# Attention's weights times values: one 32-bit product replaced by three products of 16-bit high and low parts

## The chip, the cores and the metric

The kernel runs on one core of a Trainium2 chip. A core has a matrix engine (PE, with its weight loads shown apart as PEld), a vector engine (DVE), a scalar or activation engine (ACT), a general engine (POOL), and a queue engine that starts most transfers (SP). The metric is the device time of one execution in microseconds (us); lower is better. Results of the PE go to eight PSUM banks, everything else lies in SBUF, and larger tensors in DRAM.

## What is computed

Two layers over 1024 tokens of width 1024. Each layer normalises its input, projects it (`h @ w_in`) and runs three groups of heads: a bidirectional gated delta rule (GDN, 6 heads), latent attention (MLA, 6 heads) and RWKV-7 (4 heads). Their outputs are concatenated, gated, projected by `w_out` and added to the input. The change is in the attention; cut to that part the reference reads:

```python
def mla_branch(cols, positions, q_norm_g, w_uq, kv_norm_g, w_ukv):
    ...
    kv = (rms_norm(cols['mla_ckv'], kv_norm_g) @ w_ukv).reshape(b, l, MLA_HEADS, MLA_NOPE + MLA_V)
    k_nope, v = kv[..., :MLA_NOPE], kv[..., MLA_NOPE:]
    ...
    def attend(q_blk):
        s = jnp.einsum('bqhd,bkhd->bhqk', q_blk, k)
        p = jax.nn.softmax(s, axis=-1)
        return jnp.einsum('bhqk,bkhd->bqhd', p, v)
```

## The kernel before, in words

**Two streams.** A layer's work is split in two streams that share the engines. One is the scan: first RWKV (`rwkv`, 193 rounds of the scheduler loop `chain`), then GDN (`gdn`, 279 rounds). GDN has three pairs of heads and per pair eight preparations (`gdn_prep`, with the chunk inversion `invert`, lines 904 to 985) and sixteen steps (`gdn_step`, L1106 to L1130). The other is the dense stream (`dense_work`): the input projection (`in_tiles`, L378 to L380 through the helper `mm3`), then MLA (`mla`), then the parts of the output projection that are ready (`out_part`, `out_open`). What is left of the output projection (`out_proj`) runs after both, on the whole machine.

**What sets the order.** The dense stream is a generator. Each `yield us` announces how many us of PE work the next piece is reckoned at. In every round `chain` calls `tick(dense / len(turn))` once per running thread, so that a round moves the dense stream's goal by `DENSE_R` us during RWKV and by `DENSE_G` us during GDN, and pulls pieces until the goal is reached. Whatever the dense stream has left when GDN is done is pulled at once. On top of that `order` ties PE instructions of the two streams to each other: a dense matmul stands behind the scan's last matmul of `LEAD` = 4 rounds ago, and the scan's matmuls behind the last dense one. The framework then lays out each engine's instructions in one fixed order, and every engine works through its own in that order.

**MLA.** Per layer there are six units: three pairs of heads (`pr`) times two halves of 512 queries (`nh`). A unit first gets its queries and keys (`mla_q`, `mla_k`) and the maximum of the scores (`mla_max`, L1740 on the PE and the reduction L1741 on DVE). Then `mla_main` goes over eight blocks `t` of 128 keys. For each block and each of the two heads `h`, `scores` makes a 128x512 block of scores with three matmuls (L1773 to L1775) in a bank from the pool `A`, and ACT takes the exponential (L1777, into a buffer named `mp`). POOL adds it to the running sum `acc[h]` (L1779, tiles `md`). One block later `values` multiplies: the 128x64 block of values of head `h` is the stationary operand, the 128x512 exponentials the moving one, and the two heads' results go to partitions 0 to 63 and 64 to 127 of one bank, `po`, which stays taken for the whole unit (L1784). Both operands are plain 32-bit there. `mla_tail` sums `acc` over the partitions with a matmul by ones (L1816), copies both banks out (L1818, L1819), takes reciprocals by way of DRAM, and scales (L1830, L1835). The values come from `mla_v`, which copies each projected block out of PSUM (L1685).

**Buffers.** The pool `A` has three PSUM banks, and nearly every dense matmul takes its bank there. The tag `mp` has five buffers of 128x512; `out_part` loads the residual into the same tag (L1878), adds a product to it on DVE (L1883) and stores it (L1884), 16 times a layer. In the GDN step, `gs_e` (L1111, POOL) holds the decayed state.

The middle of `mla_main` before the change, the part that the prediction speaks of most:

```python
            pT = self.T("mp", [128, 512], F32, 5)
            nc.scalar.activation(pT, ps, AF.Exp)
            if t:
                nc.gpsimd.tensor_tensor(out=acc[h], in0=prev[h] if t == 1 else acc[h], in1=pT, op=ALU.add)
            return pT

        def values(t, pT):
            for h in range(2):
                self.did = nc.tensor.matmul(po[NR[h]], lhsT=vv[:, t, 2 * pr + h], rhs=pT[h], start=(t == 0), stop=(t == 7))
```

## Time and profile before

| what | value |
|---|---|
| median of three runs | 2501.53 us (2496.85 to 2509.19) |
| the profiled execution: its own time | 2507.43 us |
| the profiled execution: span from first to last instruction | 2505.7 us |
| mean granted PE clock in it | 0.951 |
| busy: PE / DVE / ACT / POOL | 91% / 66% / 55% / 34% of the span |
| attention, layer 0 and layer 1 | about 780 to 1190 us and 2000 to 2415 us |

A row of the groups reads: line, engine, operation, tiles written and read, shapes and type, number of instructions, then busy time and the mean of one in ns, then the engine's idle time just before them and what ended it. On the PE the end of a matmul is modelled: the time that one takes from the next is the distance between their starts, which the timeline shows (its first column is the start in us, the second the duration). A 32-bit matmul appears there as two instructions, its two passes. Line numbers are those of the kernel before; the change shifts lines after 424 by three to nineteen.

### The profile page before, as it was taken

To read this page: it belongs to the slowest core of one execution; us is meant where nothing else is said; L and a number is where in the kernel's file an instruction comes from. 1 tells how busy PE (TensorE), PEld (TensorE's weight loads), DVE (VectorE), ACT (ScalarE), POOL (GpSimd) and SP (SyncE) were. 2 spreads that over 40 slices of the span, in tenths; PEclk is the share of its full clock that TensorE was granted. 3 is DMA by queue.
4 is the path that set the end of the run, shared out by engine and by line. 5 is a ranking of instruction groups with operands and counts; after the bars stand their busy time and mean duration, and the time that the engine had idled before them with its cause. 6 is when DMAs were issued, how large, how long until landed. Compare 5 with 4: busy or idle time off the path is not lost.

```text
span 2505.7 us, 54928 instructions
## 1 busy us (share of the span) xinstructions
PE 2274.3 (91%) x21524; PEld 1386.8 (55%) x21524; DVE 1643.2 (66%) x3706; ACT 1386.2 (55%) x3077; POOL 844.7 (34%) x1079
## 2 busy tenths in 40 slices
PE   5999989899899999988989999898988999998988
PEld 3455645555575555544754555555546755554556
DVE  6557778655577765775345676877456776667655
ACT  5567656655555554555245775666565456555541
POOL 1222323223224544554012232342232255445430
PEclk9999999899899989999999999998998899899999
DMA  4121222213251111102212222222224411111041
GB/s 127 46 66 51 69 64 77 56 61 120 98 171 43 37 52 31 32 25 90 93 63 56 56 68 70 66 67 56 90 88 138 128 41 32 50 38 32 21 145 68
DMA packets 140338, 174.09 MB, mean 69 GB/s; under 512 B 37072, under 2 KB 95536, under 8 KB 140080
## 3 DMA queue, kind: packets, MB, share of 16 engines
q1 hardware_dynamic: 139936, 170.19, 22.5%
q8 instruction: 170, 2.79, 0.5%
q14 instruction: 88, 0.72, 0.1%
q0 software_dynamic: 144, 0.39, 0.1%
HBM read 106.88 MB, written 39.04 MB: 58 GB/s over the span
## 4 chain that ended last, share of the span: by engine, by line
PE 56%; DVE 19%; ACT 8%; issue 6%; POOL 6%; DMA 5%; SPq 0%; POOLq 0%; ACTq 0%; DVEq 0%
PE pa L378 5%; PE pa L1784 5%; PE pa L379 5%; PE pa L380 5%; PE pb L923 4%; DMA wf<-in_w_in_dram 3%; PE pa L1740 3%; POOL wl L539 2%; PE pa L1773 2%; DVE cacc L735 2%; PE pe L840 2%; PE pe L1348 2%; PE pe L966 2%; PE pa L1774 1%; PE pc L1114 1%
## 5 line engine op out<-in xcount | busy, mean ns | idle before, releaser
L378 PE MATMUL pa<-h,wh 128*128 128x512 f16 x864 | 335.6, 388 | 1.4 <-DVE h L491 1.4
L380 PE MATMUL pa<-h,wl 128*128 128x512 f16 x864 | 333.7, 386 | 0.8 <-POOL wl L539 0.8
L379 PE MATMUL pa<-h,wh 128*128 128x512 f16 x864 | 334.5, 387 | 0.0
L949 DVE TENSOR_TENSOR z<-pb,c 128x256 f16<-128x256 f32 (+1 forms) x320 | 155.7, 487 | 166.4 <-PE pb L923 163.4
L927 ACT COPY bdz<-z 64x256 f16<-64x256 f16 (+1 forms) x384 | 173.4, 455 | 123.1 <-DVE z L949 99.3
L1779 POOL TENSOR_TENSOR md<-md,mp 128x512 f32<-128x512 f32 x144 | 192.1, 1336 | 141.6 <-ACT mp L1777 132.4
L539 POOL TENSOR_TENSOR wl<-wf,wh 128x512 f16<-128x512 f32 x108 | 128.1, 1203 | 234.8 <-ACT wh L538 200.7
L954 ACT CAST x<-pb 128x256 f16<-128x256 f32 (+1 forms) x320 | 135.1, 422 | 103.8 <-PE pb L923 102.7
L1784 PE MATMUL pa<-mp,mv 128*64 128x512 f32 x384 | 188.4, 631 | 0.0
L967 ACT CAST xT<-pe 128x512 f16<-128x512 f32 x256 | 151.1, 590 | 57.1 <-PE pe L966 56.0
L1412 POOL TENSOR_TENSOR rs_e<-rs_z,rw_em 64x128 f32<-64x128 f32 x120 | 57.2, 491 | 287.1 <-DVE rs_z L1439 257.5
L1741 DVE TENSOR_REDUCE mmx<-pa 128x1 f32<-128x512 f32 x192 | 130.9, 686 | 32.5 <-PE pa L1740 29.2
L928 DVE COPY bdz<-z 64x256 f16<-64x256 f16 (+1 forms) x384 | 139.0, 365 | 17.4 <-PE pe L966 5.7
L1777 ACT ACTIVATE mp<-pa 128x512 f32<-128x512 f32 x192 | 114.4, 596 | 63.6 <-PE pa L1775 60.3
L923 PEld LDWEIGHTS <-bdgh 128*128 128x128 f16 x1920 | 93.4, 100 | 88.8 <-issue 56.8
L923 PEld LDWEIGHTS <-xT 128*128 128x128 f16 x1600 | 77.5, 100 | 97.2 <-issue 55.8
L380 PEld LDWEIGHTS <-wl 128*128 128x128 f16 x864 | 85.2, 99 | 81.6 <-issue 6.0
L735 DVE SCALAR_TENSOR_TENSOR cacc<-raw,dv,cacc 128x512 f32<-128x512 f32 x144 | 124.1, 884 | 6.9 <-ACT raw L728 3.5
L378 PEld LDWEIGHTS <-wh 128*128 128x128 f16 x864 | 91.0, 105 | 66.0 <-issue 11.4
L923 PE MATMUL pb<-z,xT 128*128 128x64 f16 x1600 | 109.3, 197 | 16.7 <-DVE z L949 12.7
L529 DVE TENSOR_REDUCE wc<-wf 128x1 f32<-128x512 f32 x108 | 71.7, 680 | 71.8 <-DMA wf<-in_w_in_dram 71.5
L379 PEld LDWEIGHTS <-wh 128*128 128x128 f16 x864 | 85.3, 99 | 60.1 <-issue 8.4
(462 smaller groups left out, 5677.0 us busy)
## 6 DMA issues: line engine op xcount, KB each, us to landing
wf<-in_w_in_dram SPq DMA_DIRECT2D x54, 512.0 KB
q_d<-cacc SPq DMA_DIRECT2D x18, 512.0 KB
rw_ka<-rw_kr SPq DMA_DIRECT2D x32, 256.0 KB
rw_ka<-rw_ak SPq DMA_DIRECT2D x64, 128.0 KB
gate_d<-gate SPq DMA_DIRECT2D x16, 512.0 KB
wof<-in_w_out_dram SPq DMA_DIRECT2D x16, 512.0 KB
xp_d<-mp SPq DMA_DIRECT2D x32, 256.0 KB
xo<-xp_d SPq DMA_DIRECT2D x16, 512.0 KB
```

The source lines that it names most:

```text
L378: self.did = nc.tensor.matmul(out, lhsT=lh, rhs=rh, start=(first and idx == 0), stop=False)
L379: self.did = nc.tensor.matmul(out, lhsT=lh, rhs=rl, start=False, stop=False)
L380: self.did = nc.tensor.matmul(out, lhsT=ll, rhs=rh, start=False, stop=(last and idx == n - 1))
L539: nc.gpsimd.tensor_tensor(out=wl[:, ks], in0=wf[:, ks], in1=wh[:, ks], op=ALU.subtract)
L735: nc.vector.scalar_tensor_tensor(out=acc[:, c], in0=raw[:, c.start + k:c.stop + k], scalar=tap(k), in1=acc[:, c], op0=ALU.mult, op1=ALU.add)
L923: self.did = nc.tensor.matmul(ps[:, 64 * u:64 * u + 64], lhsT=st(lhsT, u), rhs=rhs(u), start=True, stop=True)
L927: nc.scalar.copy(zb[self.H[0], :, 0], t[self.H[0]])
L928: nc.vector.tensor_copy(zb[self.H[1], :, 1], t[self.H[1]])
L949: nc.vector.tensor_tensor(out=self.q8(z), in0=v(ps), in1=self.m8(self.c2(f"w{k}"), w), op=ALU.mult)
L967: nc.scalar.copy(xn[:, g:g + 4].rearrange("p u h i -> p (u h i)"), p2)
L1779: nc.gpsimd.tensor_tensor(out=acc[h], in0=prev[h] if t == 1 else acc[h], in1=pT, op=ALU.add)
L1784: self.did = nc.tensor.matmul(po[NR[h]], lhsT=vv[:, t, 2 * pr + h], rhs=pT[h], start=(t == 0), stop=(t == 7))
```

## The change

The exponentials and the values are each split in a 16-bit high part and a 16-bit low part (the remainder), and `values` makes three products instead of one: high times high, low (of the exponentials) times high, high times low (of the values), for both heads in turn. To split the exponentials, ACT takes the exponential twice, once in 32 bits and once in 16, and DVE (head 0) or POOL (head 1) subtracts. A bias of log 16 scales them up; the values are divided by a bound worked out from the weights, and `mla_tail` multiplies the bound back in. `acc[h]` takes the first block's exponentials directly, so that the first addition reads it in place. The tag `mp` goes from five buffers to two, four 16-bit buffers each are added for high and low parts, `gs_e` goes from two to one, and the values' buffer is split in two of half the width. The yield in front of `values` goes from 1.45 to 0.7 us; `DENSE_R` goes from 1.0 to 0.95 and `DENSE_G` from 1.03 to 0.9.

```diff
--- before.py
+++ after.py
@@ -220,8 +220,8 @@
 WB = 2
 W_MAX = .4
 SETS_R = 1
-DENSE_R = 1.0
-DENSE_G = 1.03
+DENSE_R = 0.95
+DENSE_G = 0.9
 LEAD = 4
 GATE = "gate"
 PAUSE = -1.0
@@ -422,6 +422,9 @@
         self.i16 = self.cp.tile([128, 64], F16, name="i16")
         nc.vector.tensor_copy(self.i16, self.c("i64"))
         self.negb = self.c2("neg")
+
+        self.ebias = self.cp.tile([128, 1], F32, name="ebias")
+        nc.vector.memset(self.ebias, math.log(16.0))
         self.wt16 = self.cp.tile([128, 2, 128], F16, name="wt16")
         nc.vector.tensor_copy(self.wt16.rearrange("p d (h i) -> p d h i", h=2),
                               self.c2("wt").unsqueeze(2).to_broadcast([128, 2, 2, 64]))
@@ -1107,7 +1110,7 @@
             r = self.T("gs_r", [128, 2, 64], F32, 2)
             nc.vector.tensor_tensor(out=r, in0=reg[:, 0], in1=self.both(s["vtok"], i), op=ALU.add)
             if i < 15:
-                se = self.T("gs_e", [128, 2, 64], F32, 2)
+                se = self.T("gs_e", [128, 2, 64], F32, 1)
                 nc.gpsimd.tensor_tensor(out=se, in0=st, in1=self.dual(self.g["eg"][:, hp], i).unsqueeze(2).to_broadcast([128, 2, 64]), op=ALU.mult)
             yield
         for p, d in quads:
@@ -1669,20 +1672,31 @@
     def mla_v(self):
 
         nc = self.nc
-        W = lambda n, dt=F32R: self.T("mp", [128, 512], dt, 5)[:, :384]
-        f, h, lo = W("f", F32), W("h"), W("l")
+        W = lambda tag, dt=F32R: self.T(tag, [128, 512], dt, 2)[:, :384]
+        f, h, lo = W("md", F32), W("mp"), W("md")
         src = self.i["w_ukv"][self.l][:, 384:768]
         nc.sync.dma_start(f, src)
         nc.scalar.copy(h, f)
         nc.gpsimd.tensor_tensor(out=lo, in0=f, in1=h.bitcast(F32), op=ALU.subtract)
-        self.mv = self.T("mv", [128, 8, 6, 64], F32, 1)
+
+        c = self.U("mvs", [128, 5], F32, 2)
+        nc.vector.tensor_reduce(out=c[:, 0:1], in_=f, axis=AX.X, op=ALU.max, apply_absolute_value=True)
+        nc.vector.scalar_tensor_tensor(out=c[:, 1:2], in0=self.par("kvg"), scalar=math.sqrt(128.0), in1=c[:, 0:1], op0=ALU.mult, op1=ALU.mult)
+        nc.vector.tensor_reduce(out=c[:, 2:3], in_=c[:, 1:2], axis=AX.X, op=ALU.max, apply_absolute_value=True)
+        yield PAUSE
+        self.col_sum(c[:, 3:4], c[:, 2:3], 1e-25, 2.0 ** -15)
+        nc.vector.reciprocal(c[:, 4:5], c[:, 3:4])
+        self.vs = c[:, 3:4]
+        self.mv = [self.T("mv" + x, [128, 8, 384], F16, 1) for x in "hl"]
         ck = self.ck
         for t in range(8):
             yield 0.6
             ps = self.A()
             ts_ = slice(128 * t, 128 * t + 128)
             self.mm3(ps[:, :384], [(ck[0][:, ts_], ck[1][:, ts_], h, lo)])
-            nc.scalar.copy(self.mv[:, t].rearrange("p a v -> p (a v)"), ps[:, :384])
+            vh, vl = self.mv[0][:, t], self.mv[1][:, t]
+            nc.scalar.mul(vh, ps[:, :384], c[:, 4:5])
+            nc.vector.scalar_tensor_tensor(out=vl, in0=ps[:, :384], scalar=c[:, 4:5], in1=vh, op0=ALU.mult, op1=ALU.subtract)
 
     def mla_q(self, pr, nh):
 
@@ -1773,15 +1787,20 @@
             self.did = nc.tensor.matmul(ps, lhsT=k[h, "h"][KX[h], ts_], rhs=q[h, "h"][KX[h]], start=True, stop=False)
             self.did = nc.tensor.matmul(ps, lhsT=k[h, "h"][KN[h], ts_], rhs=q[h, "l"][KN[h]], start=False, stop=False)
             self.did = nc.tensor.matmul(ps, lhsT=k[h, "l"][KN[h], ts_], rhs=q[h, "h"][KN[h]], start=False, stop=True)
-            pT = self.T("mp", [128, 512], F32, 5)
-            nc.scalar.activation(pT, ps, AF.Exp)
+            pT = self.T("mp", [128, 512], F32, 2) if t else acc[h]
+            nc.scalar.activation(pT, ps, AF.Exp, bias=self.ebias)
+            ph, pl = self.T("mph", [128, 512], F16, 4), self.T("mpl", [128, 512], F16, 4)
+            nc.scalar.activation(ph, ps, AF.Exp, bias=self.ebias)
+            (nc.vector, nc.gpsimd)[h].tensor_tensor(out=pl, in0=pT, in1=ph, op=ALU.subtract)
             if t:
-                nc.gpsimd.tensor_tensor(out=acc[h], in0=prev[h] if t == 1 else acc[h], in1=pT, op=ALU.add)
-            return pT
+                nc.gpsimd.tensor_tensor(out=acc[h], in0=acc[h], in1=pT, op=ALU.add)
+            return ph, pl
 
         def values(t, pT):
-            for h in range(2):
-                self.did = nc.tensor.matmul(po[NR[h]], lhsT=vv[:, t, 2 * pr + h], rhs=pT[h], start=(t == 0), stop=(t == 7))
+            for n, (a, b) in enumerate(((0, 0), (0, 1), (1, 0))):
+                for h in range(2):
+                    c = slice(128 * pr + 64 * h, 128 * pr + 64 * h + 64)
+                    self.did = nc.tensor.matmul(po[NR[h]], lhsT=vv[a][:, t, c], rhs=pT[h][b], start=(t == 0 and n == 0), stop=(t == 7 and n == 2))
 
         prev = None
         for t in range(8):
@@ -1791,7 +1810,7 @@
                 yield 0.65
                 cur.append(scores(t, h))
             if prev:
-                yield 1.45
+                yield 0.7
                 values(t - 1, prev)
             prev = cur
         self.mt = 8
@@ -1807,7 +1826,7 @@
         mix = self.mix[3 + pr]
         po, acc, last = self.mo[pr, nh]
         yield PAUSE
-        yield 1.45
+        yield 0.7
         last()
         yield PAUSE
         yield 0.95
@@ -1816,7 +1835,7 @@
             self.did = nc.tensor.matmul(ps[NR[h]], lhsT=self.c("ones"), rhs=acc[h], start=True, stop=True)
         dn, oT = self.T("md", [128, 512], F32, 2), H("oT")
         nc.scalar.copy(dn, ps)
-        nc.scalar.copy(oT, po)
+        nc.scalar.mul(oT, po, self.vs)
 
         rc, rv = [self.T("mrc", [128, 2, 4], F32, 2) for _ in range(2)]
         for h in range(2):
@@ -1874,7 +1893,7 @@
         for nh, wo in enumerate(ws):
             sl = slice(512 * nh, 512 * nh + 512)
             for t in range(8):
-                xr = self.T("mp", [128, 512], F32, 5)
+                xr = self.T("mp", [128, 512], F32, 2)
                 nc.sync.dma_start(xr, self.residual(l, t)[:, sl])
                 yield 1.4
                 ps = self.A()
```

How the change moves instructions, at three places.

**PE, the products with the values of one block** (layer 0, first unit; `mp`, `mph`, `mpl` are exponentials in 32 bits, high and low, `mv`, `mvh`, `mvl` the values, `pa` a bank of pool `A`; L966, L1114 belong to GDN). Before:

```order
L966 MATMUL pe_10013<-xT_1702_9882,bdz_980_6602 128x128
L1784 MATMUL pa_9550<-mp_9918,mv_9164 64x512
L1114 MATMUL pc_10020<-vtok_9443,gd_x_9582 64x64 x4
L1773 MATMUL pa_10030<-mq_8968,mk_9118 128x512
L1774 MATMUL pa_10030<-mq_8969,mk_9118 128x512
L1775 MATMUL pa_10030<-mq_8968,mk_9119 128x512
```

Now:

```order
L1117 MATMUL pc_10276<-gs_r_10281,gd_x_9644 64x64 x4
L1803 LDWEIGHTS mvh_9712
L1803 MATMUL pa_10104<-mph_10160,mvh_9712 64x512
L1803 MATMUL pa_10104<-mph_10228,mvh_9712 64x512
L1803 MATMUL pa_10104<-mpl_10161,mvh_9712 64x512
L1803 MATMUL pa_10104<-mpl_10229,mvh_9712 64x512
L1803 LDWEIGHTS mvl_9713
L1803 MATMUL pa_10104<-mph_10160,mvl_9713 64x512
L1803 MATMUL pa_10104<-mph_10228,mvl_9713 64x512
L1787 MATMUL pa_10367<-mq_9466,mk_9580 128x512
```

(Each product has its own load of weights ahead of it; only the first with each operand is shown.) A head's product stood mostly alone between other work; now the two heads' products alternate in longer runs. Over the program, 192 products stood in 170 runs (152 of one, 16 of two, 2 of four); now 576 stand in 213 runs: 84 of one, 39 of two, 23 of three, 12 of four, 35 of five, 18 of six and 2 of seven.

**ACT and DVE, the exponentials and their low part** (same unit; `xT`, `x`, `bdz`, `z`, `gs_s`, `gs_u`, `gs_r` are GDN's). On ACT now:

```order
L957 CAST x_1772_10214<-pb_10209 128x256
L970 CAST xT_1773_10216<-pe_10217 128x512
L1791 ACTIVATE md_10106<-pa_10223,ebias 128x512
L1793 ACTIVATE mph_10228<-pa_10223,ebias 128x512
L409 ACTIVATE mr_10196<-mr_10190 64x512
L930 COPY bdz_969_6525<-z_1780_10251 64x4x64
```

On DVE now:

```order
L952 TENSOR_TENSOR z_1764_10179<-pb_10174,c_77 128x256
L931 COPY bdz_969_6525<-z_1764_10179 64x4x64
L1794 TENSOR_TENSOR mpl_10161<-md_10105,mph_10160 128x512
L1728 TENSOR_TENSOR mr_10190<-pa_10183,mr_10189 64x512
L1729 TENSOR_TENSOR mr_10191<-pa_10183,mr_10189 64x512
L1126 TENSOR_TENSOR gs_s_10236<-pc_10165,gs_e_10172 128x128
```

Before, each pair of L1791 and L1793 was the single L1777, and DVE had no instruction of `mla_main`. The subtraction L1794 waits for the second exponential; behind it on DVE stands the scan's new state `gs_s`.

**PE, the end of a layer's scan** (layer 0; L840, now L843, turns the last GDN output; L1816, now L1835, sums the denominators; L378 with `mx` is the first matmul of `out_proj`). Before:

```order
L1775 MATMUL pa_15103<-mq_13537,mk_13384 128x512
L1784 MATMUL pa_14599<-mp_15107,mv_9164 64x512
L1816 MATMUL pa_15138<-md_14600,cst 64x512
L509 MATMUL pa_15203<-ngs_15201,cst 128x1
L840 MATMUL pe_15159<-cst,osum_12304 64x64 x16
L840 MATMUL pe_15177<-cst,osum_12304 64x64 x16
L378 MATMUL pa_15263<-mq_14690,mx_15222 128x512
```

Now:

```order
L843 MATMUL pe_15659<-cst,osum_12373 64x64 x16
L1787 MATMUL pa_15677<-mq_14317,mk_14144 128x512
L843 MATMUL pe_15688<-cst,osum_12373 64x64 x16
L1803 MATMUL pa_15351<-mph_15637,mvh_9712 64x512
L1787 MATMUL pa_15738<-mq_14319,mk_14146 128x512
L1835 MATMUL pa_15761<-md_15352,cst 64x512
L1803 MATMUL pa_15351<-mph_15744,mvl_9713 64x512
L378 MATMUL pa_15846<-mq_15422,mx_15805 128x512
```

(Rows of the same lines between these are left out.) MLA was done before the scan's last two turns; now its last blocks stand around and behind them, and the output projection follows directly. In the same way 13 groups of three projection matmuls per layer moved from ahead of the last RWKV matmul to behind it (341 groups stood ahead of it, now 328).

## The prediction

> **What bounds the kernel now.** I read the page's shares first, then the stretches in which attention runs, then the chain of waits cut to them.
>
> ```profile
> PE 2274.3 (91%) x21524; PEld 1386.8 (55%) x21524; DVE 1643.2 (66%) x3706; ACT 1386.2 (55%) x3077; POOL 844.7 (34%) x1079
> PE 56%; DVE 19%; ACT 8%; issue 6%; POOL 6%; DMA 5%; SPq 0%; POOLq 0%; ACTq 0%; DVEq 0%
> ```
> ```profile
> 175.00:640.00 465.00, 428.47 (x4532) 256.19 (x4532) 318.11 (x705) 291.87 (x640) 139.68 (x178) 0.96 0.24 70
> 780.00:1190.00 410.00, 375.17 (x3544) 209.59 (x3541) 279.25 (x597) 223.28 (x524) 206.56 (x239) 0.95 0.16 45
> 2000.00:2415.00 415.00, 385.92 (x3739) 217.57 (x3736) 289.38 (x606) 231.02 (x546) 208.54 (x245) 0.97 0.15 42
> ```
> ```profile
> by line: PE pa L1784 15.0%; PE pa L1740 6.3%; PE pb L923 5.8%; PE pa L1773 5.6%; issue 5.4%; PE pa L1774 4.0%; PE pa L1775 3.8%; PE pe L966 3.1%; DVE bdz L928 2.6%; PE pc L1114 2.6%; PE pc L1120 2.4%; PE pc L1106 2.4%; PE pe L840 2.3%; PE p
> by line: PE pa L1784 14.7%; PE pa L1740 6.9%; PE pb L923 5.8%; PE pa L1773 5.7%; issue 4.7%; PE pa L1774 4.0%; PE pa L1775 3.8%; PE pe L966 3.1%; PE pc L1114 2.7%; DVE bdz L928 2.5%; PE pc L1106 2.4%; PE pc L1120 2.4%; PE pe L840 2.3%; PE p
> ```
>
> The PE carries 56% of the chain. In the attention stretches (rows two and three: PE, PEld, DVE, ACT, POOL busy) it is busy 91 to 93% of the time, DVE 68 to 70%, ACT 54 to 56%, POOL 50%. The product that the change replaces, L1784, is the largest entry of the chain there: 15.0% of 410 us and 14.7% of 415 us, 122.5 us in all.
>
> **What the product costs.**
>
> ```profile
> 1098.86 0.48 PE L1740 MATMUL pa<-mk,mq 96*128 96x512 f32 x1
> 1099.27 1.07 PE L1784 MATMUL pa<-mp,mv 128*64 128x512 f32 x2
> 1100.28 0.49 PE L1740 MATMUL pa<-mk,mq 96*128 96x512 f32 x1
> 1154.45 0.40 PE L1774 MATMUL pa<-mq,mk 128*128 128x512 f32 x1
> 1154.68 0.40 PE L1775 MATMUL pa<-mq,mk 128*128 128x512 f32 x1
> 1156.44 1.08 PE L1784 MATMUL pa<-mp,mv 128*64 128x512 f32 x4
> 1157.45 0.29 PE L923 MATMUL pb<-x,bdgh 128*128 128x64 f16 x4
> 1175.90 1.94 PE L1784 MATMUL pa<-mp,mv 128*64 128x512 f32 x8
> 1177.67 1.96 PE L1816 MATMUL pa<-md,cst 128*64 128x512 f32 x4
> ```
> ```profile
> 104.95 0.38 PE L379 MATMUL pa<-h,wh 128*128 128x512 f16 x1
> 105.17 0.38 PE L380 MATMUL pa<-h,wl 128*128 128x512 f16 x1
> 105.38 0.38 PE L378 MATMUL pa<-h,wh 128*128 128x512 f16 x1
> ```
>
> Read the starts. One head's product alone (two passes) holds the PE 1100.28 - 1099.27 = 1.01 us. Both heads' products side by side (four passes) take 1157.45 - 1156.44 = 1.01 us as well: the two column halves of the array work at once. Eight passes take 1.77 us. With 152 runs of one product, 16 of two and 2 of four (the change's section), L1784 holds the PE 152 x 1.01 + 16 x 1.01 + 2 x 1.77 = 173 us; 122.5 / 173 = 0.71 of it is on the chain.
>
> A 16-bit product of the same width takes 0.215 us (105.38 - 105.17). No row shows two 16-bit products on the two column halves. If they pair as the 32-bit ones do, a run of n takes n/2 slots, rounded up; the 213 runs make 84 + 39 + 2 x (23 + 12) + 3 x (35 + 18) + 4 x 2 = 360 slots, 77 us. If they don't, 576 x 0.215 = 124 us. I take pairing, since nothing in the 32-bit rows depends on the type. Going from the full array to a half costs something too: L1740 to L1784 is 0.41 us where L1774 to L1775 is 0.23, so 0.18 us a run, and 43 more runs cost 8 us. Saved: 173 - 77 - 8 = 88 us of PE time, or 41 unpaired; on the chain, at 0.71, **62 us** (29 unpaired; 88 if all of it counted).
>
> **What is added.**
>
> ```profile
> L1777 ACT ACTIVATE mp<-pa 128x512 f32<-128x512 f32 x192 | 114.4, 596 | 63.6 <-PE pa L1775 60.3 <-POOL mk L1656 0.3
> L490 ACT ACTIVATE h<-pa,ngs 128x512 f16<-128x512 f32 x32 | 21.6, 686 | 12.1 <-PE pa L486 12.1
> L1779 POOL TENSOR_TENSOR md<-md,mp 128x512 f32<-128x512 f32 x144 | 192.1, 1336 | 141.6 <-ACT mp L1777 132.4 <-PE pb L923 5.0 <-ACT gs_u L1116 1.4
> L539 POOL TENSOR_TENSOR wl<-wf,wh 128x512 f16<-128x512 f32 x108 | 128.1, 1203 | 234.8 <-ACT wh L538 200.7 <-issue 33.7
> ```
> ```profile
> L1830 DVE TENSOR_TENSOR mr<-mr,md x12: 679/689/1154, 856.0 to 2425.8; 128x512 f32<-128x512 f32 x12
> ```
> ```profile
> 856.01 1.15 DVE L1830 TENSOR_TENSOR mr<-mr,md 128x512 f32<-128x512 f32 x1
> ```
> ```profile
> 855.76 1.93 POOL L918 TENSOR_TENSOR bdgl<-gd_g,bdgh 64x256 f16<-64x256 f32 x2
> ```
> ```profile
> ACT mp L1777: 0.4, 2
> ```
>
> ACT: the bias is now a tile; L490, which reads a tile of scales, has 686 ns against 596. Two of those for one of these: 192 x (2 x 0.686 - 0.596) = 149 us. DVE: head 0's 96 subtractions read two SBUF operands, as L1830 does: 0.69 us, and 1.15 us beside a busy POOL (the two timeline rows overlap); at 0.9, 86 us, and 11 us for the 16 new remainders in `mla_v`. POOL: 96 x 1.203 = 115 us by L539, the same subtraction. In all 361 us, none of it on PE. What covers it: the products come one block after their exponentials, and before, the PE waited for L1777 at L1784 only 0.4 us in all (last row; the wait list of L1784). What is behind it: GDN's casts on ACT, and on DVE the scan's `gs_s`, behind L1794. At nothing it costs 0. If it joined the chain like each engine's other work (chain over busy from the page: DVE 29%, ACT 14%, POOL 18%) it would cost 28 + 21 + 21 = 70 us. I take **30**, below the middle, since it is fed a block ahead.
>
> **The tail.**
>
> ```profile
> 1184.11 1.98 PE L840 MATMUL pe<-cst,osum 64*64 64x64 f32 x32 [4.17 <-DVE osum L1153]
> 1186.96 1.97 PE L840 MATMUL pe<-cst,osum 64*64 64x64 f32 x32 [0.88 <-ACT osq L1158]
> 1190.65 0.79 PE L378 MATMUL pa<-mq,mx 128*128 128x512 f32 x1 [1.71 <-ACT mx L406]
> ```
>
> At the end of the scan PE idles 4.17 + 0.88 + 1.71 = 6.8 us a layer; MLA's last blocks now fill this. Against it, a block there needs two additions and a subtraction on POOL, 2 x 1.34 + 1.20 = 3.9 us, and `mla_tail`'s round through DRAM ends after `out_proj` has begun; I put 3 us a layer. Together 2 x (3 - 6.8) = **-7** (bounds -14, the hole filled for nothing, to +12, three blocks a layer on POOL's clock with half hidden).
>
> **The residual's buffers.**
>
> ```profile
> 667.56 1.06 SPq L1878 DMA_DIRECT2D mp<-in_x_dram  x2
> 738.72 0.32 SPq L1884 DMA_DIRECT2D xp_d<-mp  x1
> ```
> ```profile
> 1903.36 4.68 DMA mk<-lat_d
> ```
>
> Sixteen tiles took 71 us from first load to last store, 4.4 us each. With two buffers a tile waits for load, addition (0.69) and store: at 4.68 us for each transfer, the slowest of this size (256 KB), 10.0 us over two buffers, 5.0 us a tile: 9 us a layer if this paces the stretch, with SP's other transfers queued behind. I take **+6** for both layers (0 to 18).
>
> **The rest at nothing.** The slower pacing moves 13 groups of projection, 13 x 3 x 0.215 = 8.4 us a layer, from RWKV to GDN; PE is busy 92% in both (first and second window), so it costs there what it frees here (bounds -8 to +8). `gs_e` with one buffer waits for the reader that its writer awaits already:
>
> ```profile
> L1111 POOL TENSOR_TENSOR gs_e<-gs_s,g_eg 128x128 f32<-128x128 f32 x84 | 36.8, 438 | 149.0 <-DVE gs_s L1123 148.8
> ```
>
> **The sum** against the profiled execution's own 2507.4 us: -62 + 30 - 7 + 6 = -33, 2474; the median of the runs is 5.9 us below that execution, so **2468 us**. All good ends: -88 - 14 - 8 = -110; all bad ones with pairing: -62 + 70 + 12 + 18 + 8 = +46.
>
> **The rivals.**
>
> *A. All of the PE time comes home* (12%): the added work stays hidden and the chain gains the full 88: -88 - 14 + 6, about 2405. For it: PE at 91 to 93%. Against: DVE at 68 to 70% already.
>
> *B. The 16-bit products don't pair* (14%): -29 + 30 - 7 + 6 = 0, about 2501. Against it: the four passes in 1.01 us.
>
> *C. Scores wait for the second exponential* (15%), the slower side. A bank of scores is free only after both exponentials, 0.69 us later; `po` holds one of three banks, so the PE, in order, stands before the scores L1773, and all of the scan behind it.
>
> ```profile
> PEld pa L1773 <- ACT mp L1777: 6.4, 9, 1.0
> ```
>
> Before, 9 of 96 loads in layer 0 waited so. If all 192 scores waited, 192 x 0.69 = 132 us; the gain of 62 + 7 - 6 is gone when 91 of them wait. With three quarters waiting: +99 - 63 = +36, about 2537. Against it: ACT had 45% to spare.
>
> *D. Weights are loaded in the open* (4%). Each 16-bit product loads its own weights; if these loads stood ahead of each product, 576 x (0.215 + 0.136) = 202 us, 37 more with the switches than now:
>
> ```profile
> L1784 PEld LDWEIGHTS pa<-mp,mv x384: 132/136/232, 784.1 to 2411.6; 128*64 128x64 f32 x192
> ```
>
> 37 x 0.71 + 30 - 7 + 6 = +55, about 2557. Against it: L379, L380 and L378 have different weights and start 0.215 us apart. The Trainium skill (TensorE: Matmul & The Clock Gate, Part 3, The mechanism) states the rule behind this: a weight load overlaps running matmuls only where its row group differs, and both heads use all rows. By that rule the result would be D; these rows disagree with it.
>
> **How the numbers follow.** Forecast 55%, own range 2440 to 2492. With A below, B, C and D above, the range that leaves out two in ten is 2412 to 2525. About 0.5% (12.5 us) is what a measurement here tells from no change. Faster than 2489: 0.51 of the forecast, all of A, 0.03 of B: 0.66. Same: 0.04 + 0.07 of B + 0.03 of C: 0.14. Slower: the rest, 0.20.
>
> **What would show it.** Pairs of L1803 starting some ns apart and a busy time near 80 us (else B); exponentials near 686 ns and L1794 near 0.9 us; waits of L1787 on L1793 few (else C); no hole before the second L843; the residual additions not waiting for their loads. I am wrong if L1803 shrinks as computed and the attention stretch does not.

## The result, and the profile after

The changed kernel takes 2588.55 us (median; 2585.67 to 2601.14) against 2501.53 us: a ratio of 1.036, interval 1.0335 to 1.0385. It is 87 us slower, where 33 us less were forecast and the range ended at 2525. The profiled execution took 2601.14 us; it is the slowest of the five, while that of the kernel before lies 6 us above its median. Lines of the changed kernel are numbered three to nineteen higher than before: the products are L1803, the scores L1787 to L1789, the two exponentials L1791 and L1793, the subtraction L1794, the running sum L1796.

The page of the changed kernel, busy time and the chain of waits by engine:

```profile
PE 2284.8 (88%) x21720; PEld 1418.0 (55%) x21720; DVE 1769.6 (68%) x3829; ACT 1510.2 (58%) x3269; POOL 953.6 (37%) x1175
PE 49%; DVE 22%; ACT 9%; issue 7%; POOL 6%; DMA 5%; SPq 1%; POOLq 0%; DVEq 0%; ACTq 0%
```

The PE's share of the chain fell from 56 to 49%, but its busy time rose, and DVE took over a part. Its stretches (length, then PE, PEld, DVE, ACT, POOL busy, granted clock, DMA): GDN with projection and then attention, layer 0 and layer 1.

```profile
590.00:810.00 220.00, 192.45 (x2167) 130.41 (x2165) 154.60 (x399) 122.19 (x290) 62.05 (x99) 0.92 0.33 107
810.00:1240.00 430.00, 365.28 (x3311) 214.48 (x3309) 316.54 (x580) 265.51 (x569) 256.31 (x271) 0.89 0.14 40
1870.00:2090.00 220.00, 193.31 (x2160) 130.79 (x2159) 153.90 (x398) 121.63 (x289) 61.98 (x99) 0.92 0.33 107
2090.00:2520.00 430.00, 366.37 (x3311) 215.00 (x3308) 313.02 (x576) 265.85 (x570) 255.12 (x270) 0.88 0.14 40
```

The attention stretches of before were 410 and 415 us, with the PE busy 375 and 386 us at a clock of 0.95 and 0.97. Now they are 430 us each, with 365 us busy at 0.89 and 0.88: more scan work stands ahead of them, less PE work in them, and yet they are longer. The groups of the changed kernel, the three products and the added work:

```profile
L1803 PE MATMUL pa<-mph,mvh 128*64 128x512 f16 x192 | 71.7, 433 | 10.8 <-ACT mph L1793 10.8
L1803 PE MATMUL pa<-mpl,mvh 128*64 128x512 f16 x192 | 69.1, 430 | 19.9 <-POOL mpl L1794 15.6 <-DVE mpl L1794 4.2
L1803 PE MATMUL pa<-mph,mvl 128*64 128x512 f16 x192 | 64.2, 430 | 0.0
L1793 ACT ACTIVATE mph<-pa,ebias 128x512 f16<-128x512 f32 x192 | 130.8, 684 | 0.1
L1794 POOL TENSOR_TENSOR mpl<-mp,mph 128x512 f16<-128x512 f32 x84 | 102.0, 1214 | 0.3
L1794 DVE TENSOR_TENSOR mpl<-mp,mph 128x512 f16<-128x512 f32 x84 | 78.5, 934 | 11.9 <-ACT mph L1793 11.1
```

The durations of the added work are as predicted: 684 ns an exponential, 1214 ns on POOL, 934 ns on DVE. What was wrong is what they cost.

**What the products hold.** The first two rows are a run of one product and the instruction behind it, the others a run of three pairs and the instruction behind it:

```profile
1226.51 0.40 PE L1803 MATMUL pa<-mph,mvh 128*64 128x512 f16 x1
1226.84 0.50 PE L1787 MATMUL pa<-mq,mk 128*128 128x512 f32 x1
...
1052.99 0.41 PE L1803 MATMUL pa<-mph,mvh 128*64 128x512 f16 x2
1053.23 0.38 PE L1803 MATMUL pa<-mpl,mvh 128*64 128x512 f16 x2
1053.45 0.38 PE L1803 MATMUL pa<-mph,mvl 128*64 128x512 f16 x2
1053.76 0.45 PE L1123 MATMUL pc<-gs_u,gd_kb 64*64 64x64 f32 x8
```

One slot holds the PE 1226.84 - 1226.51 = 0.33 us and three hold it 1053.76 - 1052.99 = 0.77 us: 0.22 us a slot and about 0.12 us more a run. Summed over the traces from start to start, with half-clock time counted half, L1784 held the PE 173 us before, as the prediction has it, and L1803 holds it 110 us, where the prediction has 77 + 8 = 85.

**Where the time lies.** In these traces the granted clock is 1 or 0.5 at any moment. If a matmul takes twice as long at half clock (scores below stand 1.8 times as far apart), the PE loses half of the time in which it is busy at half clock. PE work at full clock is then busy time less that, and idle is span less busy time. For the profiled executions, from their traces (the last rows are runs described below):

| kernel | span | PE idle | lost to the clock | PE work at full clock |
|---|---|---|---|---|
| before | 2505.7 | 231 | 107 | 2167 |
| changed | 2599.3 | 315 | 167 | 2118 |
| one exponential | 2471.3 | 255 | 115 | 2102 |
| added work alone | 2604.4 | 291 | 134 | 2180 |
| changed, with filler | 2576.3 | 301 | 117 | 2158 |

(Half clock lasted 245 us before and 385 us in the changed kernel, and the PE was busy in 215 and 334 of them. Counted as busy throughout, the PE work comes out as 2152 and 2092 us; some expectations below use these.) From before to changed: 49 us less PE work, 83 us more idle, 60 us more lost to the clock. The three add up to the 93.6 us between the spans by construction. The prediction had a term for the first, one too small for the second, and none for the third. This is an account with modelled ends of matmuls, not a proof of what caused what.

**A stall and what follows it**, in the changed kernel: the PE's timeline (start, duration; the three matmuls of head 0's scores, then of head 1's), then the stretches of 3.4 us around it.

```profile
1048.15 0.50 PE L1787 MATMUL pa<-mq,mk 97*128 97x512 f32 x1 [2.28 <-ACT mph L1793]
1048.49 0.40 PE L1788 MATMUL pa<-mq,mk 96*128 96x512 f32 x1
1048.72 0.40 PE L1789 MATMUL pa<-mq,mk 96*128 96x512 f32 x1
...
1049.42 0.79 PE L1787 MATMUL pa<-mq,mk 128*128 128x512 f32 x1
1050.02 0.63 PE L1788 MATMUL pa<-mq,mk 128*128 128x512 f32 x1
1050.44 0.63 PE L1789 MATMUL pa<-mq,mk 128*128 128x512 f32 x1
```
```profile
1046.00:1049.40 3.40, 1.25 (x11) 0.80 (x11) 2.82 (x4) 2.00 (x4) 1.23 (x2) 0.99 0.11 24
1049.40:1052.80 3.40, 3.40 (x27) 2.67 (x23) 1.42 (x3) 3.23 (x7) 3.10 (x3) 0.50 0.07 18
```

The PE waits 2.28 us for a bank that the second exponential still reads; ACT itself stood 0.34 us of that until L1849 gave up the `md` tile of a first exponential, which experiment 18 takes up. The next scores start 0.34 and 0.23 us apart; after 1049.4, at half clock, 0.60 and 0.42 us. The clock changes in steps of 3.41 us. Cut on these steps, the changed kernel's stretches at full clock show a rule by the PE's busy share: half clock followed all 34 with a share under 0.5, 18 of 50 from 0.5 to 0.7, none of 103 from 0.7 to 0.9, and 8 of 410 above, all of these outside attention. Of the 60 stretches before a rise, 58 had a share above 0.95. So this stall is paid for again: after it, the PE is busy for 3.40 us at half clock, which loses 1.7 us. The Trainium skill (TensorE: Matmul & The Clock Gate, Part 1, HAM oscillation) gives as its rule to avoid idle gaps longer than about 3.4 us. The trace disagrees on the length: here a gap of 2.28 us was enough, in a stretch with the PE busy 1.25 of 3.40 us.

**The end of attention** in the changed kernel, on the PE, behind the scan's last sum of squares:

```profile
1222.85 1.40 PE L843 MATMUL pe<-cst,osum 64*64 64x64 f32 x32
...
1229.55 0.38 PE L1803 MATMUL pa<-mpl,mvh 128*64 128x512 f16 x1 [1.41 <-POOL mpl L1794]
...
1231.22 1.07 PE L1835 MATMUL pa<-md,cst 128*64 128x512 f32 x2 [0.89 <-POOL md L1796]
1232.89 1.07 PE L1835 MATMUL pa<-md,cst 128*64 128x512 f32 x2 [0.60 <-POOL md L1796]
...
1235.00 0.38 PE L1803 MATMUL pa<-mpl,mvh 128*64 128x512 f16 x1 [0.82 <-DVE mpl L1794]
...
1236.17 0.50 PE L378 MATMUL pa<-mq,mx 128*128 128x512 f32 x1
```

The last blocks run on the clock of POOL and DVE. The output projection begins 13.3 us after that sum (1236.17 - 1222.85); before it was 3.7 us (1190.65 - 1186.96), and it begins 45.5 us later in all. In the 13.3 us the PE is busy 9.6, with blocks that stood ahead of the scan's end before; the other 3.7 us are the four waits shown.

### The profile page after: what moved, and what is told of

Its sections match the earlier page's. It is cut to its first block, busy times and chain, and to the rows that moved or that the text cites. A ratio compares the mean times of both kernels' runs of the same rounds, so it can differ in the third digit from the quotient of the medians.

```text
span 2599.3 us, 55788 instructions
## 1 busy us (share of the span) xinstructions
PE 2284.8 (88%) x21720; PEld 1418.0 (55%) x21720; DVE 1769.6 (68%) x3829; ACT 1510.2 (58%) x3269; POOL 953.6 (37%) x1175
## 4 chain that ended last, share of the span: by engine, by line
PE 49%; DVE 22%; ACT 9%; issue 7%; POOL 6%; DMA 5%; SPq 1%; POOLq 0%; DVEq 0%; ACTq 0%
PE pa L378 5%; PE pa L379 5%; PE pa L380 5%; PE pb L926 3%; PE pe L1351 2%; PE pa L1803 2%; DVE cacc L738 2%; PE pa L1787 2%; DVE bdz L931 2%; PE pa L1754 2%; DVE mmx L1755 2%; DMA wf<-in_w_in_dram 2%; PE pe L969 2%; DVE z L952 1%; POOL wl L542 1%
## 5 line engine op out<-in xcount | busy, mean ns | idle before, releaser
L378 PE MATMUL pa<-h,wh 128*128 128x512 f16 x864 | 337.9, 391 | 1.4 <-DVE h L494 1.4
L1796 POOL TENSOR_TENSOR md<-md,mp 128x512 f32<-128x512 f32 x168 | 232.2, 1386 | 102.1 <-ACT mp L1791 64.2
L931 DVE COPY bdz<-z 64x256 f16<-64x256 f16 (+1 forms) x384 | 154.0, 405 | 13.5 <-PE pe L962 2.1
L1791 ACT ACTIVATE mp<-pa,ebias 128x512 f32<-128x512 f32 x168 | 115.6, 688 | 80.1 <-PE pa L1789 53.4
L1415 POOL TENSOR_TENSOR rs_e<-rs_z,rw_em 64x128 f32<-64x128 f32 x120 | 50.3, 435 | 260.4 <-DVE rs_z L1442 238.3
L1793 ACT ACTIVATE mph<-pa,ebias 128x512 f16<-128x512 f32 x192 | 130.8, 684 | 0.1
L378 PEld LDWEIGHTS <-wh 128*128 128x128 f16 x864 | 90.9, 105 | 67.5 <-issue 13.9
L1787 PE MATMUL pa<-mq,mk 97*128 97x512 f32 x192 | 107.1, 558 | 22.2 <-ACT mph L1793 13.1
L738 DVE SCALAR_TENSOR_TENSOR cacc<-raw,dv,cacc 128x512 f32<-128x512 f32 x144 | 114.9, 809 | 5.7 <-ACT cacc L732 3.8
```

The costliest lines, as they stand in the source:

```text
L378: self.did = nc.tensor.matmul(out, lhsT=lh, rhs=rh, start=(first and idx == 0), stop=False)
L738: nc.vector.scalar_tensor_tensor(out=acc[:, c], in0=raw[:, c.start + k:c.stop + k], scalar=tap(k), in1=acc[:, c], op0=ALU.mult, op1=ALU.add)
L931: nc.vector.tensor_copy(zb[self.H[1], :, 1], t[self.H[1]])
L1787: self.did = nc.tensor.matmul(ps, lhsT=k[h, "h"][KX[h], ts_], rhs=q[h, "h"][KX[h]], start=True, stop=False)
L1796: nc.gpsimd.tensor_tensor(out=acc[h], in0=acc[h], in1=pT, op=ALU.add)
```

## The experiments

The medians of the kernel before lay between 2498.8 and 2505.3 us over these runs, so medians of different groups compare within about 0.3%, some 7 us. I held three theories first: W (the added work on ACT, DVE and POOL), P (the pacing numbers), C (the clock alone, following the PE's smaller load).

**1. The pacing of before in the changed kernel.** `DENSE_R = 1.0`, `DENSE_G = 1.03`.

> The changed kernel with the two pacing numbers of before (DENSE_R 1.0, DENSE_G 1.03); all else is as changed. Theory P (pacing: the slower goal lets the scan run ahead and pushes attention behind it, so the stretch where GDN runs with projection grew from 180 to 220 us a layer, and attention now ends after the scan): most of the 87 us come back, 2490 to 2515 us. Theory W (the second exponential and the subtractions hold the PE up, wherever they stand): the pacing is worth under 20 us, 2570 to 2590 us. Theory C (the PE, with less to do, is granted half its clock more often): no change in time beyond what P or W give, granted clock stays near 0.925.

Measured: 2668.32 us, ratio 1.0678 (1.0649 to 1.0707), granted clock 0.90. None of the theories: undoing the slower pacing costs 80 us more. With 0.7 us announced ahead of the products, the old numbers pack attention into fewer rounds of the scan.

**2. The new pacing alone in the kernel before.** `DENSE_R = 0.95`, `DENSE_G = 0.9`.

> The kernel before with the two pacing numbers of the change alone (DENSE_R 0.95, DENSE_G 0.9). Theory P: slower by 50 to 90 us, 2550 to 2590 us, since more of attention is left when the scan ends. Theory W: 2500 to 2520 us. Theory C: the PE's work is that of before, so the granted clock stays near 0.95 while attention runs.

Measured: 2529.96 us (2510.67 to 2536.93), ratio 1.0131 (1.0105 to 1.0156). Between P and W. The order is worth some 30 us there, beyond my bounds of -8 to +8.

**3. One exponential, no subtraction**, the three products kept.

```diff
-            pT = ... ; nc.scalar.activation(pT, ps, AF.Exp, bias=self.ebias)
-            ph, pl = ...
+            ph = self.T("mph", [128, 512], F16, 4)
             nc.scalar.activation(ph, ps, AF.Exp, bias=self.ebias)
-            (nc.vector, nc.gpsimd)[h].tensor_tensor(out=pl, in0=pT, in1=ph, op=ALU.subtract)
...
-            return ph, pl
+            return ph, ph
```

> The changed kernel with one exponential a block, straight to 16 bits, and no subtraction; the low-part product multiplies the high part once more, so the PE does the same work. It leaves out the low part of the exponentials. ACT loses 192 exponentials of 0.68 us, DVE 96 subtractions of 0.93 us, POOL 96 of 1.2 us. Theory W: nearly all of the loss comes back and the PE's saving shows, 2440 to 2500 us. Theory P: the pacing is still the changed one, so at most 30 us come back, 2555 to 2590 us. Theory C: the PE is idle as often as in the changed kernel, so the clock stays at 0.92 to 0.93, with a time above 2540 us.

Measured: 2467.87 us, ratio 0.9877 (0.9857 to 0.9898); 120.7 us less than the changed kernel. W holds, C falls: the PE does the same products and its clock is 0.945.

**4. The added work alone**, in the kernel before: the second exponential and the subtraction into tiles that nobody reads (two buffers each of the high and low parts; ACT waited 0.9 us for them in all).

> The kernel before with its 32-bit products and its pacing, plus the second exponential and the subtraction of every block (into tiles that nobody reads; the buffers of mp go from five to four and gs_e to one, to make room). Theory W: slower by about 87 us plus the products' saving on the chain, so by 100 to 150 us, 2600 to 2650 us. My prediction's term of 30 us (bounds 0 and 70): 2500 to 2570 us. Theory P: within the prediction's bounds, since no product waits for these tiles; the granted clock falls only if the PE stands still more often.

Measured: 2611.23 us, ratio 1.0447 (1.0425 to 1.047): 112 us, within W and far above my term. Their pages, one exponential first, then added work alone, each with its granted clock:

```profile
PE 2216.7 (90%) x21720; PEld 1388.8 (56%) x21720; DVE 1659.1 (67%) x3733; ACT 1408.5 (57%) x3077; POOL 812.9 (33%) x1079
core 0: 2471.3 us, clock 0.945
```
```profile
PE 2313.5 (89%) x21524; PEld 1401.7 (54%) x21524; DVE 1777.4 (68%) x3803; ACT 1503.7 (58%) x3269; POOL 963.1 (37%) x1175
core 0: 2604.4 us, clock 0.942
```

Against the first, the changed kernel is busy 102 us more on ACT, 111 on DVE and 141 on POOL (28 of these are running sums, which read 16 bits in the run with one exponential): 121 / 353 = 0.34 us of time for each us of it.

Where the PE stands for it, by the traces: from one exponential to the changed kernel its idle time before attention's own matmuls rises from 45 to 97 us, before the scan's from 136 to 148. The products themselves now wait 10.8 us for the second exponential and 19.8 us for the subtraction (the rows of L1803 above). With the added work alone, where no product reads the low part, attention's rise from 31 to 65 us and the scan's from 132 to 157.

**5. The second exponential alone** (experiment 3 with both exponentials, `pl = ph`).

> The changed kernel with both exponentials but no subtraction; the low-part product multiplies the high part again (the low part is left out). Without exponential and subtraction it took 2468 us, with both 2589 us. Theory A (the second exponential holds the score's bank for 0.69 us more and stands ahead of the scan's copies in ACT's queue): most of the 121 us stay, 2550 to 2585 us. Theory S (the subtractions on DVE and POOL): most go, 2475 to 2510 us.

Measured: 2511.87 us, ratio 1.0027 (1.0003 to 1.0051): 44 us, and with the subtractions 77 more. Just past S's bound, nearer to S.

**6. The subtractions alone**, from one 32-bit exponential.

> The changed kernel with one 32-bit exponential a block and the subtraction of a fixed 16-bit pattern from it in place of the 16-bit exponential; the three products all multiply that difference, so the high part is left out and the PE does the same work. Theory A: 2475 to 2510 us. Theory S: 2550 to 2585 us. If the two costs add, the losses of this run and of the one with the second exponential alone (each above 2468 us) add to about 121 us; if each is hidden until the other comes, both are small.

Measured: 2587.78 us, ratio 1.0321 (1.0284 to 1.0358). The losses (44 and 120 us) do not add to 121: without the second exponential the subtractions cost as much as both, so the parts of the 121 us depend on what stands beside them. All three products wait for the subtraction here (25 us in all, against 20 in the changed kernel). In this run ACT stood some 50 us before exponentials for an `mp` buffer, which experiment 12 follows up.

**7. The order of before.** Old pacing, and 1.45 us announced ahead of the products.

> The changed kernel with both pacing numbers of before and with 1.45 us announced ahead of the products, so that attention's pieces meet the same scan rounds as in the kernel before. Theory A or S with work that adds where it stands: 2580 to 2620 us, no better than the changed kernel's own order. If the order itself cost a part (with the two old numbers and the announced 0.7 us it took 2668 us, because attention was then packed into fewer rounds), that part comes back: 2540 to 2580 us. My prediction's step that an order costs in one place what it frees in another holds if it is within 10 us of 2589 us.

Measured: 2609.58 us, ratio 1.0413 (1.0378 to 1.0449): 21 us above the changed kernel, so its new order (pacing and announced time together) helps it, where the new pacing alone hurt the kernel before. What an order is worth differs between the two kernels.

**8. Two products**: one 16-bit exponential, no subtraction.

```diff
-            for n, (a, b) in enumerate(((0, 0), (0, 1), (1, 0))):
+            for n, (a, b) in enumerate(((0, 0), (1, 0))):
```

> One 16-bit exponential a block, no subtraction, and two products (high times high and high times low of the values); the low part of the exponentials is left out, and the row sums are taken of the same 16-bit exponentials. Against the run with one exponential and three products (2468 us) the PE loses 192 paired products, 96 x 0.215 = 21 us: 2440 to 2468 us by the 0.71 share of the chain (2453 us), and the granted clock stays at 0.94 to 0.95. If the PE's work no longer sets the time there, 2463 to 2473 us.

Measured: 2438.97 us, ratio 0.9736 (0.9699 to 0.9773), faster than both kernels, though it keeps less of the exponentials' precision than either. Another 29 us for 21 us of PE work: with the work beside it gone, at least all of that PE time comes home.

**9 and 10. One engine's subtractions at a time**: DVE's (head 0), then POOL's (head 1).

> The changed kernel with the subtraction of head 0 (DVE) alone; head 1's low-part product multiplies its high part again, so its low part is left out. Without subtractions it took 2512 us, with all 2589 us. Theory D (DVE's 96 x 0.93 = 89 us stand ahead of the scan's DVE work): 2555 to 2589 us. Theory O (POOL's subtractions carry the 77 us): 2512 to 2535 us.

> The counterpart: the subtraction of head 1 (POOL) alone; head 0's low part is left out. Theory D: 2512 to 2535 us. Theory O (POOL's 96 x 1.21 = 117 us delay the running sums and the scan's gs_e, and DVE's own work beside them takes longer: L931 405 ns with, 329 ns without): 2555 to 2589 us. If both halves cost the same, each run stands near 2550 us.

Measured: DVE's 2533.57 us (1.0136, 1.0109 to 1.0164), POOL's 2555.03 us (1.0217, 1.0186 to 1.0248): 22 and 43 us over the run without subtractions, 65 together against the 77 of both. Both times lie at the edge of O's ranges, so O is nearer, but both count. That POOL's subtractions cost by slowing DVE is not shown. The scan's copies of 64x256, the same instructions, in the run with one exponential and in the changed kernel:

```profile
L931 DVE COPY bdz<-z 64x256 f16<-64x256 f16 (+1 forms) x384 | 124.0, 329 | 13.3 <-PE pe L962 2.1
```
```profile
L931 DVE COPY bdz<-z 64x256 f16<-64x256 f16 (+1 forms) x384 | 154.0, 405 | 13.5 <-PE pe L962 2.1
```

But they take 370 ns with the second exponential alone (POOL busy 830 us against 813), 386 with POOL's subtractions and 382 with all of them on DVE (the next run).

**11. All subtractions on DVE** (`nc.vector` for both heads).

> The changed kernel, whole, with the subtractions of both heads on DVE. POOL loses 96 x 1.21 = 117 us, DVE gains 96 x 0.69 to 0.93 = 66 to 89 us. Theory O: faster than the changed kernel by 20 to 60 us, 2530 to 2570 us. Theory D: slower, 2600 to 2660 us.

Measured: 2591.62 us, ratio 1.0377 (1.0342 to 1.0412), the same as the changed kernel. O and D both fall as the one bottleneck: moving the work from POOL to DVE changes nothing.

**12. Four buffers of `mp`** in experiment 6.

> The run with subtractions and one 32-bit exponential (2588 us; the high part is left out there), with four buffers of mp in place of two. In that run ACT stood 24.8 us before exponentials for POOL's running sum, 15.3 us for DVE's and 10.0 us for POOL's subtraction to give up an mp buffer. Theory B (with two buffers of mp ACT waits for the readers, and the scan's copies stand behind it): these waits go and 40 to 80 us come back, 2510 to 2550 us. Theory D or O: the work itself costs, 2575 to 2590 us.

Measured: 2583.52 us, ratio 1.0331 (1.0295 to 1.0366). ACT's waits for an `mp` buffer are gone, and the time is 4 us less: they are not the cause.

**13. Filler**: four more 16-bit products a block that cancel, ahead of the product that waits.

```diff
+                for zz in self.zz if n == 1 else ():
+                    for h in range(2):
+                        nc.tensor.matmul(po[NR[h]], lhsT=zz, rhs=pT[h][0], start=False, stop=False)
```

> The changed kernel, whole, with four extra 16-bit products a block (two pairs: plus and minus 2^-10 of an identity pattern times the high part, which cancel in the sum) put ahead of the product that waits for the subtraction. They are 96 x 2 x 0.215 = 41 us of PE work at full clock. So far: PE time with the half-clock part halved is 2092 us in the changed kernel, 2152 us before; half clock 385 us against 245; idle PE 314 us against 231. Theory K (the half clock is a cost of its own that follows the PE's idle share, so that filling the gaps takes it away): half-clock time falls under 330 us and the time stays within 2565 to 2600 us in spite of the added work. Theory N (the gaps are longer than the filler, the half clock stays): time rises by 25 to 45 us, 2610 to 2635 us, granted clock 0.92 to 0.93.

Measured: 2590.37 us (2578.10 to 2610.68), ratio 1.0355 (1.0297 to 1.0413). 41 us more PE work moved the median by 2 us. Its profiled execution, which was its fastest, where the changed kernel's was its slowest:

```profile
PE 2275.1 (88%) x22104; PEld 1412.7 (55%) x22104; DVE 1770.7 (69%) x3829; ACT 1512.1 (59%) x3271; POOL 961.7 (37%) x1175
core 0: 2576.3 us, clock 0.946
```

The PE does 384 instructions more and is busy 10 us less. The mean clock of its timed executions is 0.937 against 0.927, that is 325 against 377 us of half clock, by 2 x (1 - clock) x time; K's numbers hold. Its executions differ by the clock as well: 2578 us at 0.946, 2611 us at 0.929.

**14. The waiting product last**: high times low of the values before low times high.

> The changed kernel, whole, with the product that waits for the subtraction put last of the three (high times high, high times low of the values, low times high), so the subtraction has 0.43 us more. If the subtraction costs by the PE's direct wait for it (L1803 waited 15.6 us for POOL's and 4.2 us for DVE's): 10 to 20 us faster, 2568 to 2580 us. If it costs by what it delays on DVE and POOL (the scan's additions and copies, the running sums): 2580 to 2595 us.

Measured: 2584.15 us, ratio 1.0315 (1.0278 to 1.0353), 4 us below the changed kernel and inside the noise. The PE's direct wait for the subtraction only fell from 19.8 to 13.6 us, so the run does not say what the rest of it costs; it shows that the order of the three products is worth little.

**15 and 17. More and less spreading of the two-product version.**

> The run with one 16-bit exponential, no subtraction and two products (2439 us; the low part of the exponentials is left out), with 0.5 us announced ahead of the products in place of 0.7 and DENSE_G 0.87 in place of 0.9, which spreads the same attention over about as many rounds. If spreading it further still pays (the changed kernel lost 80 us when it was packed into fewer rounds): 2420 to 2435 us. If the scan's end is now followed by more attention alone: 2440 to 2455 us.

> The run with two products (2439 us; the low part of the exponentials is left out) with DENSE_G 0.93 in place of 0.9. Spreading attention further cost 12 us. If 0.9 with an announced 0.7 us lies at the best place: 2440 to 2460 us. If a little less spreading is better: 2425 to 2437 us.

Measured: 2450.94 us (0.9788, 0.9754 to 0.9822) and 2448.81 us (0.9768, 0.9732 to 0.9803). Neither beats 2438.97, and the intervals overlap.

**16. The filler with one exponential** (experiment 3).

> The filler of 41 us of PE work in the run with one exponential and no subtraction (2468 us, idle PE 255 us, half clock 274 us; the low part of the exponentials is left out). In the changed kernel the filler cost 2 us in the medians and took the half clock from 385 to 281 us. Theory K (it was paid by clock that the stalls had cost): there is less half clock to win here, so the time rises by 15 to 40 us, 2483 to 2508 us. Theory G (the filler is free wherever PE has idle time, and the clock is an accident of that profile): 2465 to 2478 us.

Measured: 2480.51 us (2465.29 to 2487.38), ratio 0.9887 (0.9834 to 0.994): 13 us for 41, between K and G. The mean clock rose from 0.948 to 0.9545, from 258 to 226 us of half clock. By this reckoning the filler gave back half of 52 and half of 32 us by the clock, 26 and 16 us; the rest lay in idle time. The clock is a part of the account, not all of it, and no run changed it alone.

**18. The first exponential in its own buffer** (experiment 5 with four buffers of `mp`, none in `md`).

```diff
-            pT = self.T("mp", [128, 512], F32, 2) if t else acc[h]
+            pT = self.T("mp", [128, 512], F32, 4)
```

> The run with both exponentials and no subtraction (2512 us; the low part of the exponentials is left out), with four buffers of mp and the first block's exponential in mp again, as in the kernel before, and not in the running sum's own tile md. In that run ACT stood 9.5 us before first exponentials until the tail's last multiplication (L1849) gave up its md tile, and DVE stood 33 us at that multiplication for its transfer through DRAM; with one exponential, which does not use md, the latter was 3.9 us in the first attention stretch. Theory M (the tile md couples a unit's first exponential to the tail of the unit before): these waits go and 20 to 40 of the 44 us between 2468 and 2512 us come back, 2472 to 2492 us. Theory A (the second exponential itself costs 44 us): 2500 to 2515 us.

Measured: 2493.58 us, ratio 0.9956 (0.994 to 0.9973). 18 of the 44 us come back, just short of M; 26 us stay with the second exponential's work. The wait of the first exponentials for L1849 is gone, DVE's for the transfer is still 23 us.

## Why the prediction was wrong

- **The step that failed is the term for the added work.** I put 361 us of it at 30 (0 to 70), since the products are fed a block ahead. Its price was 121 us with the change's products, 112 us with the old ones. My upper bound took each engine's average share of the chain, 70 / 361 = 0.19; here 1 us more of it cost 0.34. What the runs show in place of "fed a block ahead": the PE waits 31 us at the products alone, where it waited 0.4 us before. Against the run with one exponential, the 128 us between the profiled spans are 60 us of idle PE (52 before attention's matmuls, 12 before the scan's, 4 less elsewhere), 52 us of clock and 16 us of PE work at full clock, of which 14 are the products, in 214 runs against 182. The amount of work, 359 us against before by the pages, came out partly by luck: ACT gained 124 us and not 149, DVE 126 and not 97.
- By parts, over the run with one exponential: second exponential 44 us (18 of them by where the first exponentials and the buffers of `mp` lie), then DVE's subtractions 22 and POOL's 43, or 77 for both. In another order the parts differ: the subtractions without the second exponential cost 120.
- **The PE's saving** was put at 88 us at full clock and is 173 - 110 = 63. The slip is in the sum: the 1.01 us of a 32-bit run holds the ends of that run, the 0.215 us of a 16-bit product was read inside a run, and I charged ends to 43 runs where all 213 have them (213 x 0.12 = 26 us). At 0.71 on the chain 63 us would be 45. What reached the end without the added work is 31 us, with the new pacing in it; -62 - 7 + 6 was predicted for those terms. No run has one exponential with the old pacing. So of the 121 us between forecast and result, 91 are the added work and about 32 these terms, less 3 us between the medians of the kernel before.
- **Pairing** held. In the rows of 1052.99 to 1053.45 above each x2 is the products of the two heads, started 3 ns apart by the trace, and the pairs follow 0.24 and 0.22 us apart, with weight loads of their own. Rivals B and D are out, though D's time (2557) is the nearest to the result.
- **Rival C** had the sign, but not the price. The waits of the scores for the exponentials, changed kernel, then before:

```profile
PEld pa L1787 <- ACT mph L1793: 20.4, 25, 3.3
PE pa L1787 <- ACT mph L1793: 13.1, 12, 3.0
```
```profile
PEld pa L1773 <- ACT mp L1777: 12.7, 18, 1.0
PE pa L1773 <- ACT mp L1777: 3.9, 8, 0.6
```

  The matmuls' waits rose from 3.9 to 13.1 us, those of their weight loads from 12.7 to 20.4 (one stall can stand in both rows, so they do not add), and a single one now lasts up to 3.3 us. These are some of the long stalls, 12 and 25 of 192, not three quarters of all scores.
- **The pacing at nothing** was wrong in size and in form: the two numbers alone lost about 30 us in the kernel before; in the changed one they and the announced time together gain about 20.
- **The tail** came near its term. From the hole before the scan's first sum of squares to the output projection the PE idles 2.0 + 3.7 = 5.7 us in layer 0, against 6.8 before, and 4.2 against 7.0 in layer 1: 4 us less, where 7 less were forecast. There is no hole before the second L843, and the waits for POOL and DVE are 3.7 us in layer 0, where 3 were put. **The residual's buffers** cost less than put: the additions (L1902) waited 4.0 us for transfers in all.
- The test that I set (L1803 shrinks as computed and the attention stretch does not) is nearly what happened: the products shrank by 63 of the 88 us computed, and the attention stretches grew from 410 and 415 to 430 us.

What stays open is how much of a stall's price is the clock: the account says 60 of 143 us, the filler shows that some of it can be had back, and neither isolates it. Why the subtractions cost as much alone as with the second exponential is open too.

## What to carry to other kernels

Where one engine is busy 90% and takes two streams in one order, do not price work added to the engines that feed it at their average share of the chain or below, even if its own results are needed a block later: here it cost 0.34 us a us, against an average of 0.19 and 0.08 assumed. Price short runs of matmuls with their ends, read from rows of the same kind of run. A saving on the bound engine counts only if its suppliers don't get slower by it. The cheap experiment is to add the feeders' work alone, into tiles that nobody reads.

## What the hardware showed that I had not expected

- A 3.4 us stretch in which the PE was busy 1.25 us was followed by one at half clock, in which scores took 0.60 and 0.42 us instead of 0.34 and 0.23. In the changed kernel's trace a busy share under 0.5 always led to half clock (34 of 34 stretches), one from 0.7 to 0.9 never did (0 of 103). Half clock in all rose from 245 to 385 us though the PE had less to do.
- 16-bit products of 512 columns on the two column halves of the array share a slot of 0.22 us, and a run of them costs about 0.12 us more, whatever its length (0.33, 0.55 and 0.77 us for one, two and three slots).
- 41 us of PE work added in the gaps cost 2 us in one kernel and 13 us in another, with the granted clock higher in both.
- DVE's copies of 64x256, the same instructions, took 329 to 405 ns in these runs, and POOL's busy time alone does not set it (370 ns at 830 us, 382 ns at 851 us, 405 ns at 954 us).
